# A diffusion block's first projection chunk in a written order, with part of its weights on GpSimd's queue

## The chip, the cores and the metric

The kernel runs on one NeuronCore of a Trainium2 chip. The metric is the device time of one execution in microseconds (us); the time shown is the median of three runs. The profile is of a further execution of the same program.

## The reference

One layer of a diffusion block over 512 latent tokens of width 2048 with 256 context tokens, all in fp32. Cut to what matters here:

```python
mod_l = (silu(c) @ w_ada + b_ada)          # 6 x 2048 numbers: shift, scale, gate of two halves
mod_c = (silu(c_ctx) @ w_ada + b_ada)
sh_a, sc_a, gt_a, sh_f, sc_f, gt_f = split(mod_l, 6)
h_l = rms_norm(x, g_mix_norm) * (1 + sc_a) + sh_a
h_c = rms_norm(ctx, g_mix_norm) * (1 + csc_a) + csh_a
... = split_projection(h_l @ w_in)          # 2048 -> 31 tiles of 128 columns: queries, keys, conv
...                                         # attention over latent + context, short conv
x = x + gt_a * merge_heads(att_l, conv_l, g_mix_out, w_out)
hf = rms_norm(x, g_ffn_norm) * (1 + sc_f) + sh_f
x = x + gt_f * conv_ffn(hf, w_up, ..., w_down)
return rms_norm(x, g_final)
```

## The kernel before

**Data.** Everything is kept transposed: x lies as 16 tiles of 128 features by 512 tokens. Every fp32 matrix is split in two fp32r parts, a rounded high part (`A.copy`, a cast on ACT; names end in h) and the remainder (`V.tensor_tensor` subtract on DVE, a "low"; names end in l). A product is three matmuls, high by high (L187), low by high (L188), high by low (L189), on one 128x128 block of weights by 512 tokens.

**Modulation.** One tile of `mod` (128 of the 12288 numbers) is a dot product of each row of a 128x2048 tile of w_ada with silu(c). DVE does it in two halves of 128x1024 (L241), each loaded by one DMA of 512 KB into a tile `ada` (four buffers, name in the profile `ada<-in_w_ada`); `total` (L235) adds the halves and the bias. Tile 16+j is the scale and tile j the shift of x's tile j. `prep(j)` does both dots, multiplies x by the reciprocal root (`rl`), applies scale and shift on ACT and splits the result into `h{j}h`, `h{j}l`. The modulation tiles 32 to 87 ("late", `late_dot`, L263) are not needed by the first projection; they are taken during attention and the output projection, the last of them at its end.

**The first projection.** k, the 16 tiles of h, is taken in three chunks, KCH = [2, 4, 10]. In a chunk the first G = 6 column tiles are done k by k (`first_banks`; weights `rf`, `wf`, outputs `pf`), the other 25 one after another (weights `rw`, `w_`, outputs `pp`, PSUM slots by `bank`). `evac` copies the outputs of the first chunk to `acc` on ACT (L539) and adds those of the later ones on DVE (L541). A list `todo` says behind which column tile of a chunk the next `prep` is written. In the third chunk a generator `ctx_mods` adds the same dots for the context (L530), with `svc`, the silu of c_ctx.

**What sets the order.** A scheduler orders each engine's instructions by dependences and its own estimate of times, except for those marked with `keep`, which stay in written order on their engine. Each engine, and each DMA queue, works strictly in its order. All loads of this part are issued by SP, in written order, so a load whose buffer is not free holds up those behind it. Two `raw` buffers of 1 MB hold weights before they are split.

**The start.** SP loads `io` (ones and the identity), c, the 16 tiles of x, c_ctx, the small vectors, and then w_ada. `silu_rows` spreads c's row over 128 partitions by matmuls with a column of ones (L413) and takes silu on ACT (L414), for c and c_ctx. The squares of x (L354) are summed on DVE (L355), the sum over features is a matmul (L316), then root, reciprocal (L291) and four transposes (L299).

## Time and profile before

| what | value |
|---|---|
| median of three runs | 2135.92 us (2135.22 to 2137.73) |
| profiled execution | 2139.37 us, span of its profile 2137.6 us |
| mean granted TensorE clock | 0.993 |
| DMA | 513.75 MB, mean 240 GB/s over the span |
| DVE dots over `ada` at L241, L530, L263 | 64, 64 and 68 of 1.22 us each |

In the profile PE is the matrix engine TensorE, PEld its weight loads, DVE VectorE, ACT ScalarE, POOL GpSimd, SP SyncE; a q behind a name is that engine's sequencer, which issues its DMAs. A row of a timeline has start, duration, engine, line, operation, output and inputs, their sizes and count, and in brackets the idle time of the engine before it with what ended it. A row of the waits has the engine and line that waited, what it waited for, the us in total, the times and the longest. The granted clock is a share of full speed; at half the clock matmuls of 512 columns start 0.43 us apart, at the full one 0.23.

### The profile page before, as it was taken

Reading aid. Unit: us, or ns where it says so; the run is one execution under the profiler, and the core shown is the slowest. Engines: PE = TensorE matmul, PEld = TensorE weight load, DVE = VectorE, ACT = ScalarE, POOL = GpSimd, SP = SyncE. Lnnn points to the kernel's source line nnn. Section 1 sums busy time; section 2 is a strip of 40 time slices with the busy share of each in tenths; the row PEclk is TensorE's granted clock in tenths of the full one; section 3 lists DMA queues with packets and bytes.
Section 4 is the critical chain, followed back from the end, with each engine's and each line's share of the span. In section 5 each row is a group of like instructions: output and inputs, shape, how many; then the busy total and the mean of one; then the engine's idle time right before and its main releaser. Section 6 shows DMA issues by size and latency. Waiting matters only on the chain.

```text
span 2137.6 us, 35318 instructions
## 1 busy us (share of the span) xinstructions
PE 2091.0 (98%) x13268; PEld 1881.8 (88%) x13268; DVE 1826.5 (85%) x3024; ACT 1047.5 (49%) x1715; POOL 117.2 (5%) x144
## 2 busy tenths in 40 slices
PE   7999999999999999999999999999999999999997
PEld 4688788888988888999999999999999889999997
DVE  7998987778896989898999999999999658888887
ACT  5533333555552337565555555555655433333445
POOL 0000000000000100011000000000000000000000
PEclk9999999999999999999999999999999999999999
DMA  8989886334459986577788888788888989878684
GB/s 331 343 279 329 276 275 195 126 128 152 166 188 353 348 283 220 142 217 207 230 238 232 233 233 244 224 234 234 235 229 229 362 306 307 250 231 239 197 236 134
DMA packets 170177, 513.75 MB, mean 240 GB/s; under 512 B 18963, under 2 KB 23315, under 8 KB 164371
## 3 DMA queue, kind: packets, MB, share of 16 engines
q1 hardware_dynamic: 133364, 418.14, 57.7%
q0 software_dynamic: 17408, 59.25, 14.1%
q10 hardware_dynamic: 19232, 34.09, 4.2%
q8 instruction: 104, 1.70, 0.3%
q14 instruction: 69, 0.56, 0.1%
HBM read 464.22 MB, written 46.14 MB: 239 GB/s over the span
## 4 chain that ended last, share of the span: by engine, by line
PE 90%; DVE 4%; DMA 3%; ACT 2%; issue 1%; SPq 0%; DVEq 0%; ACTq 0%; POOLq 0%
PE pp L187 4%; PE pp L189 4%; PE pp L188 4%; PE d L187 1%; PE o L187 1%; PE d L188 1%; PE o L188 1%; PE d L189 1%; PE o L189 1%; PE uf L187 1%; PE uf L189 1%; PE uf L188 1%; PE of L187 1%; PE of L188 1%; PE of L189 1%; PE pf L188 1%
## 5 line engine op out<-in xcount | busy, mean ns | idle before, releaser
L1151 POOL DMA_DIRECT2D u_s<-in_w_up x80 | 68.6, 857 | 684.0 <-DMA u_s<-in_w_up 378.1
L263 DVE SCALAR_TENSOR_TENSOR ada<-ada,sv 128x1024 f32<-128x1024 f32 x68 | 82.1, 1220 | 11.4 <-DMA ada<-in_w_ada 11.2
L166 ACT CAST w_0h<-rw 128x512 fp32r<-128x512 f32 (+1 forms) x63 | 38.3, 618 | 108.3 <-PE pp L188 67.6
L241 DVE SCALAR_TENSOR_TENSOR ada<-ada,sv 128x1024 f32<-128x1024 f32 x64 | 77.6, 1220 | 2.2 <-DMA ada<-in_w_ada 2.1
L530 DVE SCALAR_TENSOR_TENSOR ada<-ada,svc 128x1024 f32<-128x1024 f32 x64 | 76.0, 1219 | 2.5 <-DMA ada<-in_w_ada 2.4
L167 DVE TENSOR_TENSOR w_0l<-rw,w_0h 128x512 fp32r<-128x512 f32 (+1 forms) x63 | 42.7, 683 | 22.8 <-ACT w_0h L166 22.6
L263 DVE SCALAR_TENSOR_TENSOR ra<-ra,sv 128x1024 f32<-128x1024 f32 x44 | 52.5, 1219 | 1.1 <-DMA ra<-in_w_ada 1.1
L1265 DVE TENSOR_TENSOR u<-u,u_s 128x1024 f32<-128x1024 f32 x40 | 48.8, 1220 | 0.7 <-DMA u_s<-in_w_up 0.5
L1266 DVE TENSOR_TENSOR u<-u,u 128x1024 f32<-128x1024 f32 x40 | 48.7, 1218 | 0.0
L793 POOL TENSOR_TENSOR gr<-gr,half 128x8 f32<-128x8 f32 x4 | 10.1, 2524 | 630.1 <-DVE gr L792 538.2
L764 ACT CAST pth<-t 128x384 fp32r<-128x384 f32 x64 | 28.6, 485 | 26.4 <-PE t L761 26.4
L1075 DVE TENSOR_TENSOR tp<-a,tp 128x256 fp32r<-128x256 f32 x90 | 37.7, 419 | 3.3 <-ACT tp L1074 3.3
L1074 ACT CAST tp<-a 128x256 fp32r<-128x256 f32 x90 | 35.7, 403 | 5.5 <-DMA yl6h<-y_d 4.2
L1038 ACT ACTIVATE g<-g 128x512 f32<-128x512 f32 x43 | 27.3, 634 | 18.3 <-DVE g L1032 18.0
L541 DVE TENSOR_TENSOR acc<-acc,pp 128x512 f32<-128x512 f32 x50 | 34.1, 683 | 2.1 <-PE pp L189 2.1
L765 DVE TENSOR_TENSOR ptl<-t,pth 128x384 fp32r<-128x384 f32 x64 | 33.2, 550 | 2.6 <-ACT pth L764 2.6
L745 DVE TENSOR_REDUCE mn<-s 128x1 f32<-128x768 f32 x32 | 30.4, 953 | 4.9 <-PE s L734 4.6
L1030 ACT ACTIVATE g<-cg,sm 128x512 f32<-128x512 f32 x40 | 32.6, 815 | 0.0
L1030 ACT ACTIVATE a<-ca,sm 128x512 f32<-128x512 f32 x40 | 32.1, 802 | 0.0
L748 ACT ACTIVATE p<-s,mn 128x768 f32<-128x768 f32 x32 | 29.3, 916 | 1.6 <-DVE mn L745 1.3
L1031 DVE SCALAR_TENSOR_TENSOR g<-cg,sm,g 128x511 f32<-128x511 f32 x40 | 29.8, 746 | 0.0
L1032 DVE SCALAR_TENSOR_TENSOR g<-cg,sm,g 128x511 f32<-128x511 f32 x40 | 29.8, 746 | 0.0
(10238 smaller groups left out, 8925.0 us busy)
## 6 DMA issues: line engine op xcount, KB each, us to landing
ada<-in_w_ada SPq DMA_DIRECT2D x196, 512.0 KB, 5.7
u<-in_w_up SPq DMA_DIRECT2D x120, 512.0 KB, 8.9
w<-t_d SPq DMA_DIRECT2D x161, 256.0 KB, 5.3
u_s<-in_w_up SPq DMA_DIRECT2D x80, 512.0 KB, 4.0
u_s<-in_w_up POOLq DMA_DIRECT2D x80, 512.0 KB, 9.6
t_d<-tp ACTq DMA_DIRECT2D x126, 256.0 KB, 5.9
v<-in_w_dnw SPq DMA_DIRECT2D x72, 384.0 KB, 5.1
ra<-in_w_ada SPq DMA_DIRECT2D x22, 1024.0 KB, 4.8
```

Source lines behind the costliest of these rows:

```text
L166: A.copy(out=hi[:, :n], in_=raw[:, a:a + n])
L167: V.tensor_tensor(out=lo[:, :n], in0=raw[:, a:a + n], in1=hi[:, :n].bitcast(F32), op=ALU.subtract)
L187: PE.matmul(ps, w[0], x[0], start=first, stop=False, skip_group_check=on_top)
L188: PE.matmul(ps, w[0], x[1], start=False, stop=False, skip_group_check=on_top)
L189: PE.matmul(ps, w[1], x[0], start=False, stop=last, skip_group_check=on_top)
L241: V.scalar_tensor_tensor(out=r, in0=r, scalar=1.0, in1=vec[:, i * 1024:(i + 1) * 1024], op0=ALU.mult, op1=ALU.mult, accum_out=col[:, i:i + 1])
L263: keep(V.scalar_tensor_tensor(out=r, in0=r, scalar=1.0, in1=svs[i], op0=ALU.mult, op1=ALU.mult, accum_out=lc[:, t % 4:t % 4 + 1] if i else ...
L530: keep(V.scalar_tensor_tensor(out=raw[q], in0=raw[q], scalar=1.0, in1=svc[:, q * 1024:(q + 1) * 1024], op0=ALU.mult, op1=ALU.mult, accum_o ...
L1030: A.activation(u, src, AF.Identity, bias=s("fb", m), scale=s("fw", 86 + m))
L1151: G_.dma_start(r[-1], src[more], accum_op=ALU.add)
L1265: V.tensor_tensor(out=a11, in0=a11, in1=s1, op=ALU.add)
L1266: V.tensor_tensor(out=a12, in0=a12, in1=a11, op=ALU.add)
```

## The change

1. *The start is written out.* `io` and c are loaded from ACT's queue, c_ctx's row is not loaded and not spread here, SP starts with x and has one w_ada half between x11 and x12. The squares are summed in two parts (x0 to x13, x14 and x15); the dots of tiles 16 and 0 lie between and behind them; x0 is scaled straight from the PSUM bank `rs`. 35 matmuls whose result nobody reads (onto a bank `idle`) are put on PE between the squares and ahead of the first projection matmul.
2. *Chunk 0 is written out.* GCH = [8, 6, 6]: eight column tiles are done k by k, 23 behind them. `groups` lists 16 groups of up to four weight blocks; each is cast and split (`cast_group`, w0 to w15) up to three groups ahead of its matmuls, the outputs of a group are copied behind the next group's matmuls, and `preps` gives one or two steps of the preparation of h2 to h5 per group. Everything there is marked `keep`. Six matmuls with a zero weight stand ahead of the first matmul with h1.
3. *GpSimd's queue.* The weights of the rest of chunk 0 and all of chunk 1 (12 DMAs) are issued by GpSimd, which first makes a small copy of mod's tile 17 (`late`). SP has only w_ada and a few others there. The buffers stay two.
4. *The context's row* is spread by one DMA (`partition_broadcast`) in chunk 1, and its silu is one ACT instruction of 128x2048. It replaces eight matmul records and four silu instructions at the start.
5. *Six of the late modulation tiles* (12 dots, 6 MB of loads) are taken in the third chunk, at its last column tiles, so the output projection's end has 12 fewer.
6. The context's dots take their double step at i % 4 == 2 instead of 0, the constants `kc` are loaded in the middle of chunk 1, and the store `sv_d` (1 MB, in the profile at 16.22 us on SP) is written into the third chunk.

Three places show what moves. First DVE at the start, from the last sums of squares on (xs: squares of x; ada: dots; mod: their totals; rr: the reciprocal root; the last row is the low of h0). Before:

```order
L355 TENSOR_TENSOR xs0t<-xs0t,xs_184 128x512
L455 TENSOR_SCALAR sm<-sm 128x4
L355 TENSOR_TENSOR xs0t<-xs0t,xs_189 128x512
L241 SCALAR_TENSOR_TENSOR ada_227,dvl_231<-ada_227,sv 128x1024
L241 SCALAR_TENSOR_TENSOR ada_229,dvl_231<-ada_229,sv 128x1024
...
L291 RECIPROCAL rr<-rr 128x4
L167 TENSOR_TENSOR wf_0l<-rf_251,wf_0h 128x512
L167 TENSOR_TENSOR wf_4l<-rf_251,wf_4h 128x512
L167 TENSOR_TENSOR wf_8l<-rf_251,wf_8h 128x512
L435 TENSOR_TENSOR xr_113<-xr_113,rl 128x512
L241 SCALAR_TENSOR_TENSOR ada_283,dvl_287<-ada_283,sv 128x1024
L338 TENSOR_TENSOR h0l<-xr_113,h0h 128x512
```

After:

```order
L544 TENSOR_TENSOR xs_163<-xs_163,xs_215 128x512
L471 SCALAR_TENSOR_TENSOR ada_138,dv_218<-ada_138,sv 128x1024
L544 TENSOR_TENSOR xs_231<-xs_231,xs_235 128x512
L471 SCALAR_TENSOR_TENSOR ada_149,dv_218<-ada_149,sv 128x1024
...
L562 RECIPROCAL rr<-rr 128x4
L471 SCALAR_TENSOR_TENSOR ada_153,dv_250<-ada_153,sv 128x1024
L566 TENSOR_TENSOR xr_114<-xr_114,rs 128x512
...
L707 TENSOR_TENSOR w0l<-rf_155,w0h 128x512
L471 SCALAR_TENSOR_TENSOR ada_270,dv_291<-ada_270,sv 128x1024
L493 TENSOR_TENSOR h0l<-xr_114,h0h 128x512
```

A dot now stands between the last two sums, and between the reciprocal and the scaling of x0 stands one dot in place of three lows of weights.

Second, ACT where chunk 0 goes over into chunk 1 (copies to acc free PSUM banks; wf from rf are chunk 1's first weights; h5h is the high part of h5). Before:

```order
L166 CAST wf_0h<-rf_717 128x512
L438 ACTIVATE xr_142<-xr_142,mod,sc_861 128x512
L166 CAST wf_4h<-rf_717 128x512
L539 COPY acc_606<-pp_4_591 128x512
L539 COPY acc_619<-pp_6_612 128x512
L539 COPY acc_628<-pp_25_621 128x512
L337 CAST h5h<-xr_137 128x512
L166 CAST wf_8h<-rf_717 128x512
L539 COPY acc_665<-pp_26_658 128x512
L166 CAST wf_0h<-rf_767 128x512
```

After:

```order
L717 COPY acc_705<-pp_25_665 128x512
L174 CAST wf_0h<-rf_755 128x512
L174 CAST wf_4h<-rf_755 128x512
L174 CAST wf_8h<-rf_755 128x512
L174 CAST wf_0h<-rf_805 128x512
L174 CAST wf_4h<-rf_805 128x512
L486 ACTIVATE xr_124<-xr_124,mod,sc_711 128x512
L488 CAST h5h<-xr_124 128x512
L717 COPY acc_733<-pp_26_690 128x512
L717 COPY acc_735<-pp_26_690 128x512
L717 COPY acc_744<-pp_28_719 128x512
```

The casts of both chunk-1 loads (rf_755, rf_805) and h5's two steps now stand together, ahead of the last copies of chunk 0.

Third, DVE at the end of the output projection (ol: its outputs; ada: late dots; fq0t: the sum of squares for the next norm; hf0l: the low of the next stage's first operand). Before:

```order
L263 SCALAR_TENSOR_TENSOR ada_7408,mod<-ada_7408,sv 128x1024
L355 TENSOR_TENSOR fq0t<-fq0t,fq_7508 128x256
L291 RECIPROCAL rr<-rr 128x2
L263 SCALAR_TENSOR_TENSOR ada_7410,lc<-ada_7410,sv 128x1024
L268 TENSOR_TENSOR mod<-mod,lc 128x4
L269 TENSOR_TENSOR mod<-mod,sm 128x4
L980 SCALAR_TENSOR_TENSOR x_7267<-ol_7264,mod,x_7267 128x256
L957 TENSOR_TENSOR x_6494<-x_6494,rl 128x256
L957 TENSOR_TENSOR x_6500<-x_6500,rl 128x256
L355 TENSOR_TENSOR fq0t<-fq0t,fq_7603 128x256
```

After:

```order
L1213 SCALAR_TENSOR_TENSOR x_7337<-ol_7335,mod,x_7337 128x256
L365 TENSOR_TENSOR fq0t<-fq0t,fq_7550 128x256
L1190 TENSOR_TENSOR x_6576<-x_6576,rl 128x256
...
L1195 TENSOR_TENSOR hf0l<-x_6576,hf0h 128x256
...
L1213 SCALAR_TENSOR_TENSOR x_7339<-ol_7336,mod,x_7339 128x256
L1195 TENSOR_TENSOR hf2l<-x_6589,hf2h 128x256
L1190 TENSOR_TENSOR x_6603<-x_6603,rl 128x256
L292 SCALAR_TENSOR_TENSOR fs_7989<-mod,sm 128x1
L365 TENSOR_TENSOR fq0t<-fq0t,fq_7645 128x256
```

The dots are gone from there. The next stage's first operands (hf0l, hf2l, of the first half of the tokens) are now made ahead of the last x and its fq0t; on PE the two transposes of the reciprocal that they need stood behind the last matmul of the last `ol` tile, and now stand behind its twelfth of 48.

The diff, cut to its core:

```diff
+GCH = [8, 6, 6]
...
-    def first_banks(nm):
-        turn[:] = 5, None
+    def first_banks(nm, n):
+        turn[:] = (5 if n == 6 else 0), None
...
-    def load(src, n, name):
+    def load(src, n, name, E=None, halves=False):
...
+        if E is not None:
+            keep(E.dma_start(raw[:, :n], src))
...
+        ahead_of = deque((t, i) for j in range(NK) for t in (16 + j, j) for i in range(2))
...
-        SP.dma_start(io, consts[:, KCW:])
-        silu_rows(c, sv, "c")
...
+        A.dma_start(io, consts[:, KCW:])
+        cps = broadcast_row(c, "c")
+        keep(A.activation(tiny(1, "silu"), eps, AF.Silu))
...
+        while len(xs) < 12:
+            x_load_in()
+        ada_half()
+        while len(xs) < NK:
+            x_load_in()
...
+        parts = []
         for j in range(NK):
...
+            keep(A.activation(q, xs[j], AF.Square))
+            if j in (0, 14):
+                parts.append(q)
+            else:
+                keep(V.tensor_tensor(out=parts[-1], in0=parts[-1], in1=q, op=ALU.add))
...
+            if j == 13:
+                dot(16, 0)
+                warm_up(4)
+                sums(parts[0], True, False)
+                warm_up(3)
+            elif 8 <= j:
+                warm_up(2)
+        keep(A.activation(tiny(1, "root"), eps, AF.Sqrt))
+        sums(parts[1], False, True)
...
+        dot(16, 1)
+        dot(0, 0)
+        warm_up(1)
+        keep(V.reciprocal(rr, rr))
+        for g in range(4):
+            keep(PE.transpose(rs[:, 512 + g * P:512 + (g + 1) * P], bc(rr[:, g:g + 1], P), ident))
+        warm_up(7)
+        dot(0, 1, lambda: keep(V.tensor_tensor(out=xs[0], in0=xs[0], in1=rs[:, 512:], op=ALU.mult)))
...
-        todo = {(0, 1 + 6 * i): [(prep, 2 + i)] for i in range(4)}
...
+        def cast_group(i):
+            ci, bs, off, size, b = stream[i]
+            if off not in raws:
+                raws[off] = load(w_in[:, off:off + size * P], size * P, f"rw{off}", G_)
...
+            keep(A.copy(out=hi[:, :n], in_=src))
...
+        one = preps([1])
...
+        todo = preps(range(2, 6))
...
+        for i, (ci, bs, off, size, b) in enumerate(stream):
...
+                keep(G_.tensor_copy(out=tiny(1, "late"), in_=mod[:, 17:18]))
+            else:
+                for n in range(len(ready), min({2: 4}.get(i, i + 3), len(stream))):
+                    split_group(n)
+                if i == 2:
+                    for _ in range(6):
+                        keep(PE.matmul(banks[0, ORDER[0]], zero, warm, start=False, stop=False))
...
+            for key in out_of:
+                evac_now(*key, banks.pop(key))
+            if ci == 0 and i >= 2:
+                for _ in range(1 + (i % 3 != 0)):
+                    if not {2, 3, 4, 5} <= done:
+                        next(todo)
...
+        def context_row(i):
+            if i == 0:
+                keep(SP.dma_start(svc, c_ctx[0].partition_broadcast(P)))
...
+            else:
+                keep(A.activation(svc, svc, AF.Silu))
+                keep(SP.dma_start(kc, consts[:, :KCW]))
...
+        todo[1, 13] = [(context_row, 0)]
+        todo[1, 19] = [(context_row, 1)]
...
-                    raw = load(w_in[:, off:off + 2 * G * P], 2 * G * P, f"rf{ci}{q}")
+                    raw = load(w_in[:, off:off + 2 * G * P], 2 * G * P, f"rf{ci}{q}", G_ if ci == 1 else None)
...
-                    raw = load(w_in[:, off:off + k * P], k * P, f"rw{ci}_{m}")
+                    raw = load(w_in[:, off:off + k * P], k * P, f"rw{ci}_{m}", G_ if ci == 1 else None)
...
-                    for q in range(2 if i % 4 == 0 else 1):
+                    for q in range(2 if i % 4 == 2 else 1):
                         next(cm, None)
+                    if i == 18:
+                        late_load(ada_load)
+                        keep(SP.dma_start(sv_d, sv))
+                    elif i > 18:
+                        late_both(ada_load if i < len(ORDER) - G - 1 else None)
...
-    SP.dma_start(sv_d, sv)
```

More of the change, by code (lines that the diff above doesn't have):

```diff
@@ new lines, in block_kernel @@
+        cps = broadcast_row(c, "c")
+        keep(A.activation(tiny(1, "silu"), eps, AF.Silu))
+        A.copy(out=ones_r, in_=ones)
+        while len(xs) < 12:
+            x_load_in()
+        ada_half()
+        while len(xs) < NK:
+            x_load_in()
+        fetch_to(sm[:, :112], small[:, :112])
+        for _ in range(3):
+            ada_half()
+        raw0 = load(w_in[:, :2 * GCH[0] * P], 2 * GCH[0] * P, "rf00", halves=True)
+        warm = t2([P, T], F32R, "warm")
+        keep(V.tensor_copy(out=warm, in_=xs[0]))
@@ new lines, in block_kernel, with warm_up, sums @@
+        zero = t2([P, T], F32R, "zero")[:, :P]
+        keep(V.tensor_scalar(zero, ones, scalar1=0.0, scalar2=None, op0=ALU.mult))
+        rs = big("rs")
+        idle = big("idle")
+        def warm_up(n):
+            for _ in range(n):
+                keep(PE.matmul(idle[:, :512], ones_r, warm, start=True, stop=True))
+        def sums(q, first, last):
+            for g in range(4):
+                keep(PE.matmul(rs[:, g:g + 1], q[:, g * P:(g + 1) * P], ones[:, 0:1], start=first and g == 0, stop=last and g == 3))
@@ L457, in block_kernel @@
+        sc0 = tiny(1, "sc0")
+        keep(V.scalar_tensor_tensor(out=sc0, in0=mod[:, 16:17], scalar=1.0, in1=s("g_mix", 0), op0=ALU.add, op1=ALU.mult))
+        for _ in range(4):
+            ada_half()
+        n = GCH[0] * P
+        fetch_to(raw0[:, n:2 * n], w_in[:, n:2 * n])
+        fetch_to(sm[:, 112:], small[:, 112:])
         qan, kvl, krl, kvc, krc = [], [], [], [], []
@@ new lines, in split_group, with evac_now @@
+        def split_group(i):
+            cast_group(i)()
+        def evac_now(ci, m, ps):
+            if ci == 0:
+                acc[m] = t2([P, T], F32, f"acc{m}")
+                keep(A.copy(out=acc[m], in_=ps))
+            else:
+                keep(V.tensor_tensor(out=acc[m], in0=acc[m], in1=ps, op=ALU.add))
+        one = preps([1])
+        split_group(0)
+        scaled(0)
+        keep(A.copy(out=rl, in_=rs[:, 512:]))
+        next(one)
+        low(0)
+        split_group(1)
+        todo = preps(range(2, 6))
@@ new lines, in block_kernel @@
+        for key in full:
+            evac_now(*key, banks.pop(key))
+        for _ in todo:
+            pass
+        def context_row(i):
+            if i == 0:
+                keep(SP.dma_start(svc, c_ctx[0].partition_broadcast(P)))
+                keep(V.tensor_scalar(s("g_q", 0, 4), s("g_q", 0, 4), scalar1=-SCALE, scalar2=None, op0=ALU.mult))
+            else:
+                keep(A.activation(svc, svc, AF.Silu))
+                keep(SP.dma_start(kc, consts[:, :KCW]))
+        todo = {}
```

163 lines of the change are left out of this document (131 added, 32 removed).

## The prediction

> **What bounds the kernel now.** I read the page first: the busy times of the engines and the chain that ended last.
>
> ```profile
> PE 2091.0 (98%) x13268; PEld 1881.8 (88%) x13268; DVE 1826.5 (85%) x3024; ACT 1047.5 (49%) x1715; POOL 117.2 (5%) x144
> PE 90%; DVE 4%; DMA 3%; ACT 2%; issue 1%; SPq 0%; DVEq 0%; ACTq 0%; POOLq 0%
> ```
>
> PE sets the end; only stretches in which it waits or runs slowly can be won. Next the table by stretches (columns: us, PE, PEld, DVE, ACT, POOL, clock, DMA share, GB/s), first the start, then the third chunk.
>
> ```profile
> 0.00:50.00 50.00, 37.19 (x98) 21.87 (x99) 36.98 (x71) 28.85 (x49) 0.20 (x4) 1.00 0.89 329
> 50.00:60.00 10.00, 6.86 (x22) 4.67 (x21) 8.56 (x15) 5.34 (x10) 0.00 (x0) 0.76 1.01 403
> 50.00:100.00 50.00, 43.59 (x172) 33.21 (x171) 44.44 (x89) 29.19 (x53) 0.00 (x0) 0.93 0.93 349
> 100.00:150.00 50.00, 50.00 (x217) 40.54 (x216) 50.00 (x95) 16.08 (x27) 0.00 (x0) 1.00 0.83 293
> 360.00:380.00 20.00, 20.00 (x97) 16.23 (x96) 12.79 (x23) 8.01 (x15) 0.00 (x0) 1.00 0.32 96
> 380.00:400.00 20.00, 20.00 (x94) 16.41 (x93) 17.36 (x35) 11.95 (x24) 0.00 (x0) 1.00 0.36 125
> ```
>
> From 100 us on PE is full: 217 matmuls in 50 us, 0.2304 us each. The first 100 us hold 270 records, 28 of them small start matmuls; the other 242 are worth 55.8 us. So 44 us are lost before 100 us; the later stretches quoted are full. PE's waits up to 380 us, longest groups:
>
> ```profile
> PE pp L187 <- ACT acc L539: 6.4, 6, 1.9
> PE cc L413 <- DMA cc<-in_c_ctx: 3.7, 1, 3.7
> ```
>
> PE's timeline shows where:
>
> ```profile
> 15.67 7.16 PE L413 MATMUL cc<-cc,io 1*128 1x512 f32 x8 [3.72 <-DMA cc<-in_c_ctx]
> 22.76 1.86 PE L316 MATMUL rs<-io,xs0t 128*128 128x1 f32 x8
> 25.31 1.11 PE L299 MATMUL rs<-io,rr 128*128 128x128 f32 x4 [0.68 <-DVE rr L291]
> 29.63 2.07 PE L187 MATMUL pf<-h0h,wf_0h 128*128 128x512 f32 x4 [3.21 <-ACT h0h L337]
> 34.06 0.63 PE L189 MATMUL pf<-h0h,wf_0l 128*128 128x512 f32 x1
> 34.49 0.47 PE L188 MATMUL pf<-h0l,wf_0h 128*128 128x512 f32 x1
> 34.80 0.39 PE L189 MATMUL pf<-h0h,wf_0l 128*128 128x512 f32 x1
> 35.03 0.39 PE L188 MATMUL pf<-h0l,wf_4h 128*128 128x512 f32 x1
> 54.03 0.50 PE L187 MATMUL pp<-h0h,w_0h 128*128 128x512 f32 x1 [1.91 <-ACT acc L539]
> 57.30 0.80 PE L187 MATMUL pp<-h0h,w_0h 128*128 128x512 f32 x1 [1.23 <-ACT acc L539]
> 86.18 0.39 PE L187 MATMUL pf<-h2h,wf_0h 128*128 128x512 f32 x1
> ```
>
> The context's row matmuls (15.67) hold up the sum of squares; projection begins at 29.63, at half rate (0.43 us apart) until 34.5, and is at full rate (0.23) behind that. Chunk 1 begins at 86.18 (first h2): chunk 0's 186 matmuls, 42.9 us at full rate, took 56.55. Why the copies are late, ACT and the queue show:
>
> ```profile
> 52.88 0.62 ACT L166 CAST w_0h<-rw 128x512 fp32r<-128x512 f32 x1 [5.96 <-DMA rw<-in_w_in]
> 29.25 14.62 SPq L145 DMA_DIRECT2D ada<-in_w_ada  x8
> 43.96 0.38 SPq L145 DMA_DIRECT2D rw<-in_w_in  x1
> ```
>
> SP issues weights behind ada loads that wait for free buffers: eight took 14.62 us before the weights went out. The cast waited 5.96 us for them with the copies queued behind it.
>
> **The change, part by part.** *Start.* The rows for a chain:
>
> ```profile
> 1.58 9.56 SPq L145 DMA_DIRECT2D xr<-in_xt  x16
> xr<-in_xt SPq DMA_DIRECT2D x16, 256.0 KB, 5.5
> 16.57 0.63 ACT L354 ACTIVATE xs<-xr 128x512 f32<-128x512 f32 x1 [0.17 <-DVE xs0t L355]
> 19.02 0.69 DVE L355 TENSOR_TENSOR xs0t<-xs0t,xs 128x512 f32<-128x512 f32 x1
> 19.64 1.22 DVE L241 SCALAR_TENSOR_TENSOR ada<-ada,sv 128x1024 f32<-128x1024 f32 x1
> 20.78 1.22 DVE L241 SCALAR_TENSOR_TENSOR ada<-ada,sv 128x1024 f32<-128x1024 f32 x1
> 25.07 0.18 DVE L291 RECIPROCAL rr<-rr 128x4 f32<-128x4 f32 x1 [0.20 <-ACT rr L289]
> 28.11 0.81 ACT L438 ACTIVATE xr<-xr,mod,sc 128x512 f32<-128x512 f32 x1 [1.04 <-DVE xr L435]
> ```
>
> A 512-wide step of DVE is followed 0.62 us later, a dot 1.14. x loads go out every 0.60 us. Without io and c ahead on SP, and with one ada load among them, x13 goes out at 0.75 + 14 x 0.60 = 9.15, lands at 14.65, is squared (0.63) and added (0.69) by 16.0. Dot (16,0) runs to 17.2, the last add to 17.9; dots (16,1) and (0,0) to 20.3, with the sums and root beside them; reciprocal 20.5; transposes (1.11) to 21.6, beside dot (0,1) to 21.7; scaling x0 0.69, two small steps 0.4, h0h 0.81: 23.5. For hand-overs I add 0.7 (the bracketed ones were 0.17 to 1.04): first matmul at 24.2, **-5.4**. Ends: 23.5, or 26.7 with part of the fillers running at half rate on the path. The 35 fillers cost nothing elsewhere: PE has nothing else to do; the last seven end at 23.2 (7 x 0.23 after 21.6) at full rate, 24.6 at half.
>
> *Clock.* Half rate from 29.63 to 34.5 followed a 3.21 us wait with little before; lost: 4.9 x 0.2/0.43 = 2.3 us. I take the fillers to keep the full rate. The Trainium skill ("TensorE: Matmul & The Clock Gate", "The two states you'll see") has the clock go up only after about 3.4 us of sustained work in a free-running window. By that rule two fillers per square may not count as sustained, and the sum would lack 2.3 us; this trace's 4.9 us at half rate fits a window that may be met late, and has no fillers to show it.
>
> *Chunk 0.* 186 matmuls and six of zeros at 0.2304: 44.2 us. The wait rows above go with their cause, the second slow spell too. New waits: h1 (dots (17,0) to (1,1) are five DVE steps behind h0) 0.9; the first GpSimd load, which the `late` copy holds until mod[17] is known (about 28), then 9 to 11 us (below) against a need at 37.6 (24.2, 48 matmuls, the zeros, h1): 1.0; small ones 0.6. That is 46.7 for 56.55: **-9.8** (2.3 of it the clock), chunk 1 at 70.9. DVE has 20 dots for tiles 1 to 5 (22.8), 14 lows (8.7) and the scaling (8), some 40 us of the 48 from 22.7 on: it keeps up. DMA just does: x 4.2 MB, 24 halves of 0.5 MB, weights 4.1 and 1.6, small ones 0.4, together 22.8 MB, four halves ahead 2.1; at the old rates (329 GB/s for 50 us, then 403) 24.7 MB have landed by 70.5. Ends: 44.2 (no wait), and 51 if dots starve and hold the lows behind them.
>
> *GpSimd's queue.* The transfers there, nearest rows:
>
> ```profile
> rw<-in_w_in SPq DMA_DIRECT2D x3, 1024.0 KB, 8.9
> u<-in_w_up SPq DMA_DIRECT2D x120, 512.0 KB, 8.9
> u_s<-in_w_up SPq DMA_DIRECT2D x80, 512.0 KB, 4.0
> u_s<-in_w_up POOLq DMA_DIRECT2D x80, 512.0 KB, 9.6
> L1151 POOL DMA_DIRECT2D u_s<-in_w_up x80 | 68.6, 857 | 684.0 <-DMA u_s<-in_w_up 378.1
> ```
>
> Under load, GpSimd's 9.6 stands beside SP's 8.9 for the like; I take 9.6 and 0.86 to issue, 10.5. Two raw buffers let each load start when the one before the last is split. Counting DVE's work from the low that frees a buffer to the first low out of its new load: 11, 12.2 and 10.5 us for the second and third weight load and the first of chunk 1 (six, seven, six dots, each with six steps of up to 512), but 7.3 (four and four) for the second of chunk 1 (rf_805). So that one is some 3 us late, ACT's casts of it stand ahead of four or five copies of chunk 0, and PE waits at the **seam: +3.5** (0 to +6.5, with a slow spell like the one at 57.30). The Trainium skill ("DMA: Bandwidth & Descriptors", "Issuing engines are not separate DMA queues") speaks against a gain from the move: all issuers run on the same 16 engines, only issue time is saved. By it the 5.96 us above would go only as far as it was issue order; the trace says it was (issued at 43.96, landed 8.9 later).
>
> *Rest of chunks 1 and 2.* The context's silu over 2048 columns on ACT in chunk 1 is four rows of 0.60 and two table loads of 1.28, 5 us beside ACT's 16 in 50: **+1** (0 to 3). The sv_d store, kc load and shifted context dots fall where DMA is at 0.32 to 0.83: 0; without that cover, the store's 1 MB is 2.6 us of DMA.
>
> *Third chunk's tail.* Six steps of 30 matmuls are 41.5 us; DVE is busy about 30 of them by the last two windows, and gets 12 dots of 1.14: 43.7. **+1** (0 to 3), part of it covered by DVE's lead.
>
> *End of the output projection* has twelve dots fewer:
>
> ```profile
> 811.27 1.23 DVE L263 SCALAR_TENSOR_TENSOR ada<-ada,sv 128x1024 f32<-128x1024 f32 x1 [0.80 <-DMA ada<-in_w_ada]
> 814.35 0.61 PE L316 MATMUL rs<-io,fq0t 128*128 128x1 f32 x4 [2.85 <-DVE fq0t L355]
> 815.83 0.39 PE L187 MATMUL uf<-hf0h,ufw0h 128*128 128x256 f32 x1 [0.88 <-ACT ufw0h L1023]
> ```
>
> A dot that waited for its load stands ahead of fq0t. After, x, three short steps of the next stage and fq0t remain there, 1.9 us (0.48 + 0.42 + 0.38 + 0.16 + 0.42, as such steps last in that stretch), 0.95 less than 2.85; and since hf0 is now made during the last tile, most of the 0.88 can go: **-1.5** (-4 with a slow spell behind it, to 0).
>
> **Sum**: -5.4 - 9.8 + 3.5 + 1 + 1 - 1.5 = -11.2. The profiled execution took 2139.37 (span 2137.6), 3.45 above the median of the runs; it becomes 2128.2, the median 2135.92 becomes **2124.7**. A measurement tells 0.2%, 4.3 us, from no change.
>
> **Rivals.**
> *DVE or DMA gives the gain back.* From 100 to 150 DVE was full, 50.00 of 50. Its idle time from 8.7 to 100 was about 10.7 us (13.0 + 5.6 less 7.9 at the start), and its first dot comes 3.6 earlier. If DMA, at 0.93 from 50 to 100, lets only a third of that idle time go, and the added casts cost 1, DVE reaches chunk 1's end 6.2 earlier, and the sum is -6.2 + 2 - 1.5 = -5.7: **2130.2**. For it: the full DVE. Against: PE's waits there name no DVE row of size.
> *More is won.* No wait at the seam, silu and tail hidden, start at 23.6: -6 - 10.2 - 1.5 = -17.7: **2118.2**. For it: DVE finishes h5 well before PE ends chunk 0; against: rf_805's late buffer.
> *The fillers don't hold the clock*: -8.9, **2127.0**.
> *GpSimd's loads are late (slower).* If GpSimd's loads get half of the engines while SP's ada loads run, a 1 MB load takes twice 8.9, 18.7 with its issue. With L from release to landing, DVE waits four times, L less 11, 12.2, 10.5 and 7.3, less the three groups (8.3 us) that casts run ahead of PE: 25.5 at 18.7, against 15.7 won without any load wait (11.2 + 3.5 + 1.0): +9.8, **2145.7**. It decides from L = 16.3. For it: DMA at 0.93 to 1.01 there. Against: SP's 8.9 was taken at that share too, and the 9.6 beside SP's loads. The page on DMA of the Trainium skill ("SWDGE vs HWDGE vs iDMA") says that GpSimd's descriptors can be held up by DVE's use of SBUF; DVE is full here, but the 9.6 was with DVE busy as well.
>
> **How the numbers follow.** Forecast case (gain 8 to 15, 2121 to 2128) 0.51; gain given back 0.18, a third of it within 0.2%; more won 0.16; clock not held 0.06; late loads 0.09, two thirds of it slower. Faster: 0.51 + 0.12 + 0.16 + 0.06 = 0.85; same 0.09; slower 0.06. The range 2116 to 2132 leaves out the late loads and the ends of two cases, about 0.16.
>
> **What would show it.** First matmul of h0 near 24, 0.23 apart at once; h2's first near 71; the copies' 6.4 us gone from PE's waits, a new wait on ACT at the seam; the wait of 2.85 near 1.9. Wrong if GpSimd's weight loads take over 16 us, if PE waits for DVE's lows between 100 and 180, or if PE has gaps at 350 to 390.

## The result and the profile after

The changed kernel took 2150.68 us (median of six runs, 2149.05 to 2154.23), the kernel before 2136.38 beside it (2134.61 to 2137.73): a ratio of 1.0069 [1.0056, 1.0082]. The change makes it slower by 14.7 us of the first median; 11.2 of gain were forecast.

The page of the kernel after, busy times and the chain that ended last:

```profile
PE 2096.0 (97%) x13303; PEld 1883.8 (88%) x13303; DVE 1822.5 (85%) x3025; ACT 1048.8 (49%) x1715; POOL 124.5 (6%) x157
PE 83%; DVE 6%; DMA 5%; issue 4%; ACT 1%; POOL 0%; DVEq 0%; POOLq 0%; ACTq 0%; SPq 0%
```

PE still sets the end, but its share of the chain fell from 90% to 83%. PE's timeline of the kernel after at the places that the prediction named:

```profile
24.42 1.19 PE L763 MATMUL pf<-h0h,w0h 128*128 128x512 f32 x4 [0.49 <-ACT h0h L485]
25.44 1.10 PE L763 MATMUL pf<-h0h,w0l 128*128 128x512 f32 x4
73.48 0.40 PE L195 MATMUL pf<-h2h,wf_0h 128*128 128x512 f32 x1
81.23 0.80 PE L195 MATMUL pf<-h4h,wf_0h 128*128 128x512 f32 x1 [3.86 <-ACT wf_0h L174]
420.34 2.08 PE L389 MATMUL qr<-xq,kc 128*128 128x512 f32 x2 [5.28 <-ACT xq L885]
827.63 0.61 PE L326 MATMUL rs<-io,fq0t 128*128 128x1 f32 x4 [1.65 <-DVE fq0t L365]
```

The first matmul with h0 stands at 24.42 (29.63 before) and at full rate at once, four in 1.02 us. Chunk 1 begins at 73.48 instead of 86.18. So 12.7 us were won by then, and then more was lost. The table by stretches shows where (columns as before):

```profile
0.00:50.00 50.00, 41.06 (x152) 28.75 (x153) 36.63 (x69) 31.25 (x56) 3.04 (x8) 1.00 0.90 327
50.00:100.00 50.00, 45.47 (x181) 35.08 (x181) 43.52 (x88) 25.47 (x46) 2.65 (x5) 0.93 0.86 312
100.00:150.00 50.00, 49.53 (x214) 39.85 (x213) 50.00 (x97) 19.28 (x28) 2.13 (x4) 1.00 0.83 298
250.00:300.00 50.00, 46.39 (x192) 36.73 (x191) 40.40 (x83) 16.68 (x33) 0.00 (x0) 0.93 0.74 253
400.00:450.00 50.00, 43.34 (x268) 37.95 (x268) 35.95 (x74) 26.57 (x55) 0.00 (x0) 0.93 0.44 150
```

Before, PE was full in the fourth of these stretches and nearly so in the last (the kernel before, the same view):

```profile
250.00:300.00 50.00, 50.00 (x230) 41.02 (x229) 44.30 (x90) 17.74 (x34) 0.00 (x0) 1.00 0.81 272
400.00:450.00 50.00, 47.88 (x321) 43.16 (x320) 32.63 (x62) 28.96 (x61) 0.00 (x0) 1.00 0.35 119
```

From 250 to 300 there are 192 matmuls for 230, from 400 to 450 268 for 321. PE's longest groups of waits in the projection up to 400 us, after:

```profile
PE pp L195 <- ACT w_0h L174: 6.3, 6, 1.9
PE pf L195 <- ACT wf_0h L174: 3.9, 1, 3.9
PE pp L197 <- DVE w_0l L175: 2.4, 2, 2.1
PE pp L763 <- ACT acc L717: 2.0, 1, 2.0
```

The 6.4 us of waits for copies have become 2.0; in their place stand waits for weights that are still to be loaded, cast or split. A count of the projection's 1488 main matmuls in PE's timeline tells how far ahead each kernel is. The start of the N-th, in us:

```
N of 1488             1    186    250    558    700    900   1100   1200   last
before             29.6   87.3  102.2  173.8  206.8  256.6  304.8  329.8  404.5
before, again      29.3   85.9  100.8  172.4  205.4  255.5  303.7  327.9  402.5
after              24.4   74.2   95.5  167.8  200.8  257.4  309.1  333.5  411.9
first chunk only   24.2   71.7   91.4  163.7  196.7  252.1  300.4  327.3  401.5
```

"First chunk only" is the kernel e7 of below. Chunk 0 is the first 186. "Before, again" is a second profile of the same kernel (e15). After leads the kernel before by 13.1 us there, by 6.7 at the 250th, is 0.8 behind at the 900th, and 7.4 behind at the end of the projection; the query's projection behind it costs it 6.5 more (first scores at 450.9, before 437.0).

### The profile page after: what moved, and what is told of

The parts are those of the page before. It is cut to its first block, busy times and chain, and to the rows that moved or that the text cites. A ratio compares the mean times of both kernels' runs of the same rounds, so it can differ in the third digit from the quotient of the medians.

```text
span 2152.1 us, 35376 instructions
## 1 busy us (share of the span) xinstructions
PE 2096.0 (97%) x13303; PEld 1883.8 (88%) x13303; DVE 1822.5 (85%) x3025; ACT 1048.8 (49%) x1715; POOL 124.5 (6%) x157
## 3 DMA queue, kind: packets, MB, share of 16 engines
q1 hardware_dynamic: 131776, 407.90, 55.6%
q0 software_dynamic: 19072, 70.40, 15.6%
## 4 chain that ended last, share of the span: by engine, by line
PE 83%; DVE 6%; DMA 5%; issue 4%; ACT 1%; POOL 0%; DVEq 0%; POOLq 0%; ACTq 0%; SPq 0%
PE pp L195 3%; PE pp L197 3%; PE pp L196 3%; DMA rw<-in_w_in 2%; PE o L196 1%; PE o L197 1%; PE o L195 1%; PE d L195 1%; PE d L196 1%; PE d L197 1%; PE of L195 1%; PE of L196 1%; PE uf L195 1%; PE of L197 1%; PE uf L197 1%
## 5 line engine op out<-in xcount | busy, mean ns | idle before, releaser
L273 DVE SCALAR_TENSOR_TENSOR ada<-ada,sv 128x1024 f32<-128x1024 f32 x68 | 81.8, 1218 | 4.5 <-DMA ada<-in_w_ada 4.4
L174 ACT CAST w_0h<-rw 128x512 fp32r<-128x512 f32 x50 | 30.9, 620 | 112.2 <-DMA rw<-in_w_in 52.6
L249 DVE SCALAR_TENSOR_TENSOR ada<-ada,sv 128x1024 f32<-128x1024 f32 x40 | 48.2, 1217 | 0.0
L175 DVE TENSOR_TENSOR w_0l<-rw,w_0h 128x512 fp32r<-128x512 f32 x50 | 34.2, 685 | 16.0 <-ACT w_0h L174 16.0
L1026 POOL TENSOR_TENSOR gr<-gr,half 128x8 f32<-128x8 f32 x4 | 10.1, 2526 | 499.7 <-DVE gr L1025 499.7
L998 DVE TENSOR_TENSOR ptl<-t,pth 128x384 fp32r<-128x384 f32 x64 | 33.5, 548 | 3.4 <-ACT pth L997 3.4
L994 PE MATMUL t<-io,p 128*128 128x128 f32 x192 | 28.2, 273 | 2.0 <-DVE ptl L998 2.0
L1263 DVE SCALAR_TENSOR_TENSOR g<-cg,sm,g 128x511 f32<-128x511 f32 x40 | 29.8, 745 | 0.0
```

What stands on the lines that cost most here:

```text
L249: ins = V.scalar_tensor_tensor(out=r, in0=r, scalar=1.0, in1=vec[:, i * 1024:(i + 1) * 1024], op0=ALU.mult, op1=ALU.mult, accum_out=col[:, ...
L273: keep(V.scalar_tensor_tensor(out=r, in0=r, scalar=1.0, in1=svs[i], op0=ALU.mult, op1=ALU.mult, accum_out=lc[:, t % 4:t % 4 + 1] if i else ...
```

## The experiments

### Which part costs: e1 to e4

I split the change into its first chunk, the two edits in the third chunk, and the late tiles put alone into the kernel before.

**e1_no_late**: after, with all late tiles back at the output projection.

```diff
-                        late_load(ada_load)
                         keep(SP.dma_start(sv_d, sv))
-                    elif i > 18:
-                        late_both(ada_load if i < len(ORDER) - G - 1 else None)
```

> The changed kernel without the six late modulation tiles in the third chunk (all 56 are taken where they were before); all else as changed. In the two profiles the changed kernel leads by 12.7 us at chunk 1's start, by 5.9 at chunk 2's, by 10 at its first column tile, is 4.2 behind at the eleventh, 7.4 behind at the last, 13.9 behind at the first attention scores, 14.5 at the end. Theory L (the six tiles are the cost: DVE and SP's queue are full at the third chunk's end): what is lost from the eleventh tile on, 3 + 6.5, comes back and the output projection's end gives 2 back: about 2143. Theory Q (SP's order in the third chunk's first half, which holds weights behind runs of w_ada loads, is the main cost): only the tail after the third chunk comes back, 2144 to 2146, and the loss between the first and the eleventh tile, 14 us, stays. Theory C (the cadence of the context's dots): 2150, no change.

2143.02 us (2140.8 to 2145.4), ratio 1.0032 [1.0019, 1.0044].

**e2_cadence0**: after, the context's dots with their double step where they had it before.

```diff
-for q in range(2 if i % 4 == 2 else 1):
+for q in range(2 if i % 4 == 0 else 1):
```

> The changed kernel with the context's double steps back at i % 4 == 0; late tiles stay. Theory C: the 14 us lost between the third chunk's first and eleventh tile go: about 2137. Theories L and Q: within 3 us of 2150, since the run of seven w_ada loads ahead of one weight load stands in this order too.

2148.77 us, ratio 1.0051 [1.0038, 1.0064].

**e3_third_as_before**: after with both of these edits.

> The changed kernel with both taken back: the third chunk as before, apart from the store of sv_d. Theory L or C, or both: the lead of 5.9 us at chunk 2's start is kept, about 2130. Theory Q: the weights are still behind w_ada in the third chunk's first half, 2140 to 2144.

2138.47 us (2134.78 to 2143.49), ratio 1.0015 [1.0005, 1.0026].

**e4_before_late**: the kernel before, with the six late tiles in the third chunk.

```diff
+                    if i == 18:
+                        late_load(ada_load)
+                    elif i > 18:
+                        late_both(ada_load if i < len(ORDER) - G - 1 else None)
                     if i >= 5 and i % 2 == 1 and (i - 5) // 2 < CTX_EARLY:
```

> The kernel before with the six late tiles in the third chunk and nothing else of the change. Theory L: the tail costs here what it costs there, 9.5 less 2 won at the output projection's end: 2143 to 2145. Theory Q: the tail was late only since the third chunk was late: 2133 to 2138.

2144.8 us, ratio 1.0036 [1.0023, 1.0048].

By the ratios, of 2135.9 us, the late tiles cost 7.9 (after against e1), 7.7 (e2 against e3) and 7.7 (e4 alone): three times the same, in either surrounding. The moved double step costs 3.6 (e1 against e3) and 3.8 (after against e2). The first chunk with GpSimd's queue, e3, costs 3.2 where it should have won. 7.9 + 3.6 + 3.2 = 14.7 gives the whole result; that sum must come out, since each step starts where the last ended. What speaks for separate costs is that each came out alike in another surrounding. By the means of the runs on the one chip that e1 to e4 shared, the late tiles cost 9.3 +- 3.0 (e2 less e3) and 8.3 +- 2.7 (e4 less before), the double step 4.3 +- 2.7 (e1 less e3).

Where the late tiles hurt, DVE's timeline of the kernel after shows:

```profile
403.24 1.22 DVE L273 SCALAR_TENSOR_TENSOR ada<-ada,sv 128x1024 f32<-128x1024 f32 x1
413.69 1.22 DVE L273 SCALAR_TENSOR_TENSOR ada<-ada,sv 128x1024 f32<-128x1024 f32 x1
```

They did not fit into the third chunk, whose last column tiles they were written at. The last four of the twelve run at 403 to 416, two of them behind the last projection matmul (411.9), and the query's rotation (`rope`, the matmul `qr`) waits. It waits through ACT, which is held by a step for the context (`cr`) that stands behind the two dots on DVE; ACT's copy `xq`, which the rotation needs, comes behind it at 419.71. ACT's timeline of after:

```profile
417.63 1.09 ACT L634 ACTIVATE cr<-cr,modc,scc 128x256 f32<-128x256 f32 x2 [2.16 <-DVE cr L633]
```

PE's timeline at this place, of e4 and then of e1:

```profile
413.75 2.08 PE L379 MATMUL qr<-xq,kc 128*128 128x512 f32 x2 [4.71 <-ACT xq L656]
```

```profile
409.17 1.13 PE L389 MATMUL qr<-xq,kc 128*128 128x512 f32 x2 [0.97 <-ACT xq L882]
```

With the late tiles the wait is 4.71 (5.28 in after) and the two matmuls behind it last 2.08, half rate; without them 0.97 and 1.13. The gain for which they were moved is there: from the first output-projection matmul to the first of the up-projection it is 26.40 us in after and e4, 27.98 before (28.84 in its second profile).

For the double step I looked at ACT's waits for the weights' loads. ACT's waits from 200 to 400 us, kernel before, then after:

```profile
ACT w_0h L166 <- DMA rw<-in_w_in: 23.1, 8, 4.7
```

```profile
ACT w_0h L174 <- DMA rw<-in_w_in: 50.1, 12, 9.8
```

In e1 it is 40.7, in e2 44.9, in e3 33.5: 5 to 7 us less with the old step. But the second profile of the kernel before has 12.9 for 23.1, so such sums move by 10 us between two executions. Nor does a long run of `ada` loads on SP ahead of a weight load tell the two apart: seven loads take 13.54 us from 219.18 in after, and 13.53 from 219.13 in e3. That the step's new place costs time is shown by the times; how it does so stays open.

### The first chunk: GpSimd's queue and the seam, e5 to e8

e3's 3.2 us can be the queue, the seam, or a lead that is lost later. My theory was the seam and the hand-over from GpSimd's queue to SP's in the third chunk.

**e5_third_gpsimd**: e3, with the third chunk's weights on GpSimd's queue too.

```diff
-..., G_ if ci == 1 else None)
+..., G_)
```

> e3 (the written first chunk, third chunk as before; 2138.5 us) with the weights of the third chunk on GpSimd's queue as well, so SP carries only w_ada and the context there. In e3's profile the lead over the kernel before is 12.5 us at chunk 1's start, 5.7 at chunk 2's, 2.4 at its sixth column tile, 1.4 at its last. Theory Q (weights stand behind w_ada loads on SP): the lead of 5.7 is kept through the third chunk, 2133 to 2135. Theory D (DVE's work for the context, not the queue, sets the third chunk's pace): 2137 to 2140. GpSimd's slower issue costs: above 2140.

2142.97 us, ratio 1.0041 [1.0027, 1.0055]: not faster than e3 but slower, so taking these loads off SP's queue brings nothing. Whether a price of GpSimd's queue hides a small gain this run can't tell.

**e6_svc_raw**: e3, where chunk 1's second load has a buffer of its own (`svc`, not in use yet).

```diff
+                    if (ci, q) == (1, 2):
+                        raw = svc
+                        keep(G_.dma_start(svc[:, :2 * G * P], w_in[:, off:off + 2 * G * P]))
```

> e3 with chunk 1's second load of weights (three blocks of 512 columns) going into the context row's tile svc, which is empty until later, instead of waiting for a raw buffer: it can start 11 us sooner. Theory S (the seam's late load costs the 6.8 us lost in chunk 1: 3.9 of waiting, 2 of half rate, and what follows): the lead at chunk 2's start is 11 to 12 instead of 5.7. If the third chunk passes leads on: about 2132. Theories Q and D (the third chunk has a pace of its own): the lead is there at chunk 2's start and gone at its end, 2136 to 2139.

2139.46 us (2134.72 to 2144.43), ratio 1.0025 [1.0013, 1.0036]: no gain over e3. The wait that it takes away comes back under another name, as PE's waits of e6 up to 430 us show:

```profile
PE pf L197 <- DVE wf_0l L175: 3.6, 1, 3.6
PE pp L197 <- DVE w_0l L175: 3.7, 2, 3.3
```

**e7_all_sp**: e3, all weights on SP, without the `late` copy: the written first chunk alone.

```diff
-                keep(G_.tensor_copy(out=tiny(1, "late"), in_=mod[:, 17:18]))
-..., f"rw{off}", G_)
+..., f"rw{off}")
-..., G_ if ci == 1 else None)
+...)
```

> e3 with all weights on SP's queue again, in written order, and without the small copy that holds GpSimd back: the first chunk's order alone. If the move to GpSimd's queue is what rids the first chunk of its waits: the waits for weights behind w_ada come back, chunk 1 starts 3 to 6 us later than in e3 (73.7), total 2140 to 2144. If it only moves the issue: within 2 us of e3 at chunk 1's start and in total.

2136.11 us (2131.4 to 2138.95), ratio 1.0002 [0.999, 1.0015].

**e8_both**: e5 and e6 together.

> e5 and e6 together. Theories S and Q: both leads are kept, 11 us at the end of the third chunk: 2126 to 2129. Theory D: as e6, 2136 to 2139.

2138.86 us, ratio 1.0023 [1.0012, 1.0035].

e7 speaks on the queue and the `late` copy together: with the weights back on SP and no copy, chunk 0 ends 2.7 us earlier in the profiles (186th matmul 71.7, e3 74.4), and the time is 2.8 lower by the ratios. Those two intervals overlap, but on the chip that e5 to e8 shared, 12 runs of each put the mean of e7 3.4 +- 2.2 us under e6 and 3.3 +- 2.3 under e8. The loads from 20 to 180 us, after and then e7 (median us from issue to landing at the end):

```profile
rw<-in_w_in POOLq DMA_DIRECT2D x8, 1024.0 KB, 8.3
rf<-in_w_in POOLq DMA_DIRECT2D x2, 768.0 KB, 8.4
```

```profile
rw<-in_w_in SPq DMA_DIRECT2D x8, 1024.0 KB, 7.8
rf<-in_w_in SPq DMA_DIRECT2D x7, 768.0 KB, 7.6
```

The queue saved little issue time. The first five weight loads go out at 29.45, 35.14, 48.11, 61.05 and 72.32 on GpSimd, at 28.32, 37.10, 50.06, 61.59 and 69.65 on SP: at most 2.0 us earlier, and later for the first, which the `late` copy holds, and the last, which meets the seam. How much of the cost is the copy and how much the queue, no run here shows. The Trainium skill ("DMA: Bandwidth & Descriptors", "Issuing engines are not separate DMA queues") says that all issuers end on the same DMA engines and only issue time is saved; these issue times and landings agree.

So the first chunk alone is some 15 us ahead at its end, and wins nothing in the time.

### Where the lead goes: e9 to e14

Two theories. *DVE's work*: PE runs ahead in chunk 0, but DVE has done no more work than before; PE meets it later and waits until the lead is gone. Then less work on DVE in both kernels lets the lead live. *The order of SP's loads*: then it changes little.

**e9_before_short**: the kernel before, with the second half of 20 latent dots over 8 columns of 1024; the rest of these halves is left out, and all loads stay.

```diff
+            k = 8 if t % 16 >= 6 and i else 1024
```

> The kernel before; of the latent dots of tiles 6 to 15 the second half is taken over 8 columns instead of 1024 (20 dots, some 23 us of DVE's work left out; all loads stay), so that DVE is not full from 100 to 160 us. It is the base for the next run. PE waits little there before, so theory D (DVE's backlog sets the pace up to the third chunk) and theory Q (the order of SP's queue) both expect 2131 to 2135.

2131.62 us (2127.1 to 2136.79), ratio 0.9987 [0.9975, 0.9999].

**e10_sp_short**: e7 with the same edit.

> e7 (written first chunk, all weights on SP, third chunk as before; 2136.1 us, 1.7 above the kernel before in its job) with the same 20 half dots cut to 8 columns. e7 leads by 16 us at the end of chunk 0, by 11 from the 372nd to the 700th projection matmul, by 5 at the 900th, 3 at the last. Theory D: with DVE relieved the lead that chunk 0 wins passes through: 8 to 10 us below e9, 2123 to 2126. Theory Q: the lead goes in the third chunk all the same, within 3 us of e9.

2133.36 us, ratio 0.9993 [0.9984, 1.0003].

**e11_filled**: e7 with each `low` of h one dot later and h6's steps moved into chunk 0, to fill DVE's idle time there.

```diff
-            todo = preps(range(2, 6))
+            todo = preps(range(2, 7))
...
+                        if hold:
+                            low(hold.pop())
...
-                low(j)
+                hold.append(j)
```

> e7 with all of its work, but DVE kept fuller in the written chunk: the low of h2 to h5 one dot later (DVE waited 1.5 us for ACT before each), and the dots of tile 6 taken in chunk 0 too. Theory D: DVE's backlog shrinks by 4.5 to 8 us and so does the total: 2128 to 2132. Theory Q: no change, 2135 to 2138. If the denser work makes chunk 0's own lows late: above 2138.

2137.3 us, ratio 1.0009 [1.0, 1.0018].

**e12_no_fillers**: e7 with each group of fillers cut to one matmul of 8 columns.

```diff
-            for _ in range(n):
-                keep(PE.matmul(idle[:, :512], ones_r, warm, ...))
+            for _ in range(min(n, 1)):
+                keep(PE.matmul(idle[:, :8], ones_r, warm[:, :8], ...))
```

> e7 with nearly all filler matmuls ahead of the first projection matmul left out (a few of 8 columns stand in their places). If the fillers hold the clock: the first 5 us of the projection are at half rate as before (0.43 us apart), chunk 0 ends 2.3 us later; under theory D the total does not move (within 2 us of 2136), under theory Q it rises by 2. If the clock does not depend on them: 0.23 apart from the first on.

2133.09 us (2127.15 to 2135.79), ratio 0.9992 [0.9981, 1.0003].

**e13_before_short2**: e9, and the second half of every context dot over 8 columns too.

```diff
+                    k = 8 if q else 1024
```

> e9 (the kernel before, 20 latent half dots cut to 8 columns) with the second halves of the context's 32 dots in the third chunk cut to 8 columns as well: another 36 us of DVE's work left out, between about 185 and 350 us. All loads stay. The base for the next run. PE waits some 2 us there in the kernel before: 2129 to 2133 under every theory.

2134.98 us (2129.46 to 2138.26), ratio 0.9991 [0.9981, 1.0001].

**e14_sp_short2**: e10 with that edit.

> e10 (written first chunk, weights on SP, 20 latent half dots cut) with the same cut of the context's dots. Theory D2 (the lead of chunk 0 is lost where DVE is full: at the seam and in 100 to 160, and again among the context's dots at 200 to 230, which e10 had left whole): with both relieved the lead passes, 8 us or more below e13. Theory Q (the order of SP's queue, which is the same here): within 3 us of e13. If the lead is at the third chunk's end in the profile and not in the times, it is lost behind it.

2129.71 us (2125.7 to 2132.89), ratio 0.9973 [0.9963, 0.9983].

With the latent dots alone relieved, e10 is not faster than e9, though in the profiles its last projection matmul comes at 394.1 against 402.2. In the same two profiles 7.8 of this is left at the first scores, 6.1 at the first up-projection matmul and 2.7 at the end, so most of it is lost far behind the projection. (The execution profiled for e9 took 2136.6 us, 5 above its median, so even this end flatters e10.) With the context's dots relieved too, e14 is 5.3 us faster than e13 by the medians (means: 4.4 +- 2.2, 10 and 11 runs on one chip), and its last projection matmul stands at 392.8 against 400.3. In e7 the same stretches looked like this (100 to 160 and 200 to 230 us), then in e14:

```profile
100.00:160.00 60.00, 59.53 (x256) 47.96 (x255) 60.00 (x117) 21.07 (x30) 0.00 (x0) 1.00 0.84 297
200.00:230.00 30.00, 26.18 (x107) 20.80 (x106) 28.92 (x56) 7.78 (x14) 0.00 (x0) 0.94 0.87 305
```

```profile
100.00:160.00 60.00, 60.00 (x259) 48.62 (x259) 51.55 (x128) 22.19 (x33) 0.00 (x0) 1.00 0.93 334
200.00:230.00 30.00, 29.02 (x130) 23.40 (x129) 24.07 (x58) 8.87 (x16) 0.00 (x0) 1.00 0.88 305
```

The fourth number is DVE's busy time: 60.00 of 60 and 28.92 of 30 in e7, where PE did 107 matmuls from 200 to 230; 24.07 in e14, where it did 130. PE's waits of e7 up to 430 us name DVE first:

```profile
PE pp L197 <- DVE w_0l L175: 4.9, 2, 3.8
PE pf L195 <- ACT wf_0h L174: 2.9, 1, 2.9
```

The places of the loss stand in the counts. Over the kernel before, e7 leads by 15.6 us at the 186th matmul, by 10.8 at the 250th (the seam is between), still by 10.1 at the 700th, by 4.5 at the 900th and by 3.0 at the last. Over e13, e14 leads by 13.2, 8.8, 8.9, 7.5 and 7.5. So what relieving DVE gives back is the loss between the 700th and the 900th, where e7's waits of 4.9 us for DVE's lows are: this part was lost to DVE's work: e14 shows it in the counts and in the time. e10 keeps most of it too (7.9 at the 900th, over e9), without being faster at the end. The loss at the seam, 4 to 5 us, stands in both, and that it is DVE's work too is argued, not shown.

Another part is lost where nothing was changed. From the first up-projection matmul to the end, the five profiles of kernels with the first chunk of before take 1316.4 to 1323.0 us, the thirteen with the written one 1321.9 to 1326.4, by the means 4 us more: about as much as was left of the lead. One stretch of 100 us there (it begins 1000 us behind that matmul), kernel before, e7 and e12:

```profile
1815.80:1915.80 100.00, 100.00 (x835) 100.00 (x834) 86.13 (x124) 38.49 (x46) 5.97 (x7) 1.00 0.82 239
1811.90:1911.90 100.00, 98.67 (x818) 97.17 (x817) 82.78 (x123) 37.61 (x45) 5.96 (x7) 1.00 0.78 228
1808.40:1908.40 100.00, 100.00 (x845) 100.00 (x844) 87.03 (x128) 39.31 (x47) 5.96 (x7) 1.00 0.81 243
```

In e7, PE waits there for DVE's lows, 1.2 us in all, and DVE for loads of `w_dnw` (weights of the feed-forward part), six times 2.3 to 2.6 us; in the kernel before the longest such wait is 1.0. All twelve profiles with the written first chunk and all of its fillers have a wait for these loads of 2.4 us or more; the five with the first chunk of before, and e12 without the fillers, none above 1.2. Why these loads land later there stays open.

So the first chunk's lead is lost in three places: at the seam, to DVE's work in the third chunk, and behind the start of the up-projection. e6 took the seam's late buffer away and won nothing, e14 tested the second, and no run tests the third. With DVE relieved, 4 to 5 us of the lead reach the time. e11 shows that filling DVE's idle time in chunk 0 only moves the loss forward (186th matmul at 78.3 for 71.7, and the time no lower); e12 belongs to the clock, below. No kernel that does all of the work is faster than the kernel before by more than its interval; the lowest, e12 at 0.9992, is within it.

### Two executions of one program: e15 and e16

**e15_before_look**: a second profile of the kernel before.

> A second profile of the kernel before, whose first was of an execution 4 us above its median. If e7's lead at the third chunk's end is 3 us only because of that execution, this one reaches the last projection matmul at 400 to 402 us instead of 404.5; if it is the rule, at 404 to 405.

**e16_sp_look**: a second profile of e7.

> A second profile of e7, for the same: the last projection matmul was at 401.5 us. If the lead of 14 to 16 us at chunk 0's end is always lost by then, it is at 400 to 403 again; if the first was a poor one, below 398.

2132.11 us and 2140.63 us, one run each; the first profiled executions of the same programs took 2139.37 and 2137.45. In e16 the 700th to 900th matmul take 55.6 us (e7 55.4, before 49.8 and 50.1): the loss is in the program. What two executions of one program differ by otherwise is told in the last section.

## Why the prediction was wrong, point by point

| step | forecast | measured |
|---|---|---|
| start (first matmul of h0 at 24.2) | -5.4 | 24.42: -5.2 |
| chunk 0 (h2 first at 70.9) | -9.8 | 73.48: -7.5 more |
| seam | +3.5 (0 to 6.5) | wait 3.86, then half rate from 81.2 to 86.1 (2.3): about +6.2 |
| rest of chunks 1 and 2 | +1 | given back, see below |
| these four together | -10.7 | +0.4, -2.1 to +3.2 (e7, without GpSimd's queue) |
| GpSimd's queue with the `late` copy | +1.0 in chunk 0, 0 beside the seam | +2.8 (e3 against e7) |
| double step at i % 4 == 2 | 0 | +3.7 |
| late tiles: third chunk's tail | +1 | +9.4 (7.8, and the 1.6 won below) |
| late tiles: end of the output projection | -1.5 | -1.6 |

*Right.* The start came within 0.2 us, by its chain of x loads, squares, dots and transposes. The copies' waits went from 6.4 us to 2.0, where all of it was to go. The seam has the mechanism that was forecast, and its size is at the upper end of its range. GpSimd's and ACT's timelines of after:

```profile
72.32 0.53 POOL L159 DMA_DIRECT2D rf<-in_w_in  x1 [10.74 <-DVE w15l L707]
```

```profile
80.56 0.62 ACT L174 CAST wf_0h<-rf 128x512 fp32r<-128x512 f32 x1 [8.66 <-DMA rf<-in_w_in]
```

The load waits for the low w15l that frees its buffer, lands 8 us later, and PE, which would have needed it at 77.4, waits until 81.23. The end of the output projection won what it should: the wait for fq0t is 1.65 (2.85 before, 1.9 forecast).

*Wrong, the first step that failed: chunk 0's gain counted as time won.* The prediction let PE's lead in chunk 0 go through to the end, since DVE "keeps up", and read DVE's state from when h5 would be ready. By its sum the four steps up to there were to win 10.7 us; e7 measures +0.4. It should have read how much work DVE has done. The same view, busy times up to 66.8 and 80.5 us, when h4's low is ready after and before; first the kernel before, then after:

```profile
0.00:80.50 80.50, 62.24 (x189) 40.36 (x190) 63.36 (x124) 45.39 (x80) 0.20 (x4) 0.96 0.88 324
0.00:66.80 66.80, 50.17 (x140) 31.16 (x141) 49.70 (x97) 37.08 (x65) 0.20 (x4) 0.95 0.90 338
```

```profile
0.00:80.50 80.50, 67.76 (x261) 48.70 (x261) 62.60 (x121) 45.40 (x82) 4.63 (x11) 0.99 0.88 317
0.00:66.80 66.80, 57.35 (x220) 41.19 (x221) 50.22 (x98) 40.30 (x72) 3.57 (x9) 1.00 0.87 315
```

At 80.5 us DVE had worked 63.36 us before and 62.60 after. h4 was ready 13.7 us earlier because work was left for later: by then DVE had worked 50.22 us instead of 63.36, with 20 dots behind it instead of 29 (9 x 1.14 = 10.3 us). With DVE full from 100 to 150 us in both, the work that was put off is not caught up with there. h15's low shows the end of it, before and after:

```profile
79.79 0.69 DVE L338 TENSOR_TENSOR h4l<-xr,h4h 128x512 fp32r<-128x512 f32 x1
196.66 0.69 DVE L338 TENSOR_TENSOR h15l<-xr,h15h 128x512 fp32r<-128x512 f32 x1
```

```profile
66.11 0.69 DVE L493 TENSOR_TENSOR h4l<-xr,h4h 128x512 fp32r<-128x512 f32 x1 [1.54 <-ACT h4h L488]
203.27 0.68 DVE L348 TENSOR_TENSOR h15l<-xr,h15h 128x512 fp32r<-128x512 f32 x1
```

h4 is 13.7 us earlier, h15 6.6 later. In e7, the written first chunk alone, h4's low stands at 63.61, 16.2 us earlier than before, and h15's at 197.27, 0.6 later: the whole of what h4 gained was put-off work. Not all of the lead goes this way; the seam and the stretch behind the up-projection's start take theirs. The rival "DVE or DMA gives the gain back" had the right engine, but let a third of DVE's idle time go; none of it went (36.98 + 44.44 = 81.4 us busy in the first 100 before, 36.63 + 43.52 = 80.2 after).

*Wrong, the second: the third chunk's tail.* The step compared 43.7 us of DVE work with 41.5 us of PE and put the overflow at 1, "covered by DVE's lead". DVE had no lead by then (in e4, without any written first chunk, the tiles cost as much), and the overflow does not end with the chunk: it runs into the query's projection, where ACT stands behind DVE's late `cr` step and PE behind ACT's copy, with a wait of 5.28 and half rate behind it. The condition stood in the prediction, "if PE has gaps at 350 to 390"; the gap came at 415 to 420, behind the window that it watched.

*Wrong, the third: two edits costed too low.* The double step was put at 0 and cost 3.7; how is open. GpSimd's queue was given 1.0 for the load behind the `late` copy and cost 2.8 with that copy. The estimate of a load's flight was 9.6 us and the measured 8.3, so the rival of late loads is not the cause.

*The clock.* The fillers do hold it, and the term of 2.3 us was worth nothing that the times show. Without them, PE's timeline of e12 begins:

```profile
25.31 2.07 PE L762 MATMUL pf<-h0h,w0h 128*128 128x512 f32 x4 [1.82 <-ACT h0h L485]
27.18 1.91 PE L762 MATMUL pf<-h0h,w0l 128*128 128x512 f32 x4
28.89 1.40 PE L762 MATMUL pf<-h0l,w0h 128*128 128x512 f32 x4
```

Four matmuls take 1.87 us where after needs 1.02, until about 29.5. (The rate is read from these distances here, since the profile's granted clock reads 1.00 at the start in the kernel before and e12 too, half rate or not.) But the 186th stands at 72.2, in e7 at 71.7, and the time is no higher (ratios 0.9992 and 1.0002, intervals overlapping). I take it that PE spends the gained time waiting for weights and dots; no run separates this from the loads of `w_dnw` that land earlier in e12.

## What to carry to other kernels

When an engine in front is let run ahead, compare the *work* that the engine behind it has done up to the same time, not when one of its results is ready: a result that comes earlier because other work was put behind it is a loan. Before work is moved into a gap, find what stands behind the gap on that engine and whether PE needs it at once; an overflow of a few us there costs its wait and the half rate that may follow. And take a compound change apart by single edits, in both kernels: here the late tiles and the double step cost alike in each surrounding, and the part that had been forecast to win everything won nothing. Follow a lead to the end of the program, too: a part of this one went more than a millisecond behind the change.
